# Rotary embedding: the first store queued after half, not a quarter, of the last load

## The chip, the core and the metric

The kernel runs on one core of one Trainium2 chip. The metric is the device time in microseconds (us) from start to end of the program. The core has five engines; this kernel computes on VectorE (DVE in the profile) and a little on ScalarE (ACT). GpSimd (POOL), SyncE (SP) and ScalarE issue transfers, and 16 DMA engines carry them between the chip's main memory (HBM) and the on-chip memory of 128 partitions. TensorE is not used.

## The reference

The input `x` is float32 with 8 batches, 8 heads, 1024 positions and 64 features. Each pair of features (i, i + 32) is rotated by an angle, position times frequency i.

```python
half = x.shape[-1] // 2
angles = np.outer(positions, freqs)
cos = np.cos(angles)
sin = np.sin(angles)
x_first, x_second = x[:, :, :, :half], x[:, :, :, half:]
out_first = x_first * cos - x_second * sin
out_second = x_first * sin + x_second * cos
return np.concatenate([out_first, out_second], axis=-1).astype(np.float32)
```

The tensor is 16.8 MB and is read once and written once, so that at least 33.6 MB pass through HBM.

## The kernel before, in words

The 64 pairs of batch and head ("heads") are cut into groups. One group is 8 heads: each head's 1024 positions are cut into 16 chunks of 64 positions, and the 8 x 16 chunks fill the 128 partitions, each with one contiguous row of `run` = 64 x 64 = 4096 values. `groups` holds seven such groups (heads 8 to 63) and, last, a group of `first` = 6 heads (heads 2 to 7), which fills 96 partitions. Heads 0 and 1 (`edge` = 2) are held apart: they are loaded first, as float32, through SP's hardware queue, computed last, and stored by SP at the very end (L176).

The groups are loaded by software DMAs that POOL issues (L83). They read float32 and write bfloat16 into the tiles `xt`. The seven full groups are one load of 1024 KB each; the last group's load is cut into two loads at `cut = first_part`, the columns before the cut and the columns from it. There is one `xt` tile and one output tile `ot` for every group, so no tile is used twice and no load waits for a tile. POOL issues eight loads at once; the ninth, the second part of the last group, is issued at 11.68 us, once the first load has landed.

VectorE and ScalarE build a table of sines (with both signs) and cosines once (`tables`). Then `rotate` makes three VectorE instructions for each group: the product with the sines into `t` (L139), the product with the cosines into `ot` (L140), and the sum of `ot` and `t` with swapped halves (L142). After the third group a second, smaller table is built for the two edge heads (`turnsr`, `wholer`, `sinr`, `cosr`).

The results go out through POOL too (L152), as software DMAs that read bfloat16 and write float32, one for each group. Loads and stores of POOL are in one queue, q0, and the order is the program's. Ahead of the first store the program has POOL wait until the first part of the last load is in:

```python
nc.gpsimd.keepalive_nop(ins=[nc.gpsimd.lower_ap(xts[-1][:, :first_part])])
```

So all stores stand behind this one wait, although the first groups are computed long before it is met. The stores follow in the order of the groups, each after its group's L142. SP's two stores of the edge heads are issued once all stores but the last one have landed (`stored[:-1]`).

Of the kernel before, what the change touches and what calls it, by code (L numbers as in the profile page):

```python
# [10 lines left out]
def kernel(  # L11
# [29 lines left out]
    run = C * d  # L41
# [31 lines left out]
    nc.scalar.dma_start(out=fr[0:P:32], in_=freqs[None, :].to_broadcast([P // 32, half]))  # L73


    first_part = run // 4
    xts = []
    for lo, n in groups:
        xt = xpool.tile([P, run], bf16, name="xt")[:n * chunks]
# [130 lines left out]
```

## Time and profile before

| what | us |
|---|---|
| median of 6 runs | 86.17 |
| the six runs | 86.51, 86.58, 84.47, 85.24, 86.28, 86.07 |
| the profiled execution | 86.51 |
| its span in the trace | 84.5 |
| VectorE busy | 65.2 |
| ScalarE busy, POOL busy | 9.4, 9.4 |
| first store issued (L152) | 42.55 |
| last VectorE instruction ends (L167) | 74.1 |
| SP issues the edge heads' stores (L176) | 78.75 |

The span is the time from the first to the last record of the trace, and all times of the trace count from its start. The profiled execution took 2.0 us more than its span. Its sizes for software transfers are those of the on-chip side for loads (bfloat16, half of what HBM gives) and those of the HBM side for stores. A transfer's time to landing counts from its issue to the moment when its semaphore says that all of it is there; a transfer spreads over the 16 DMA engines and has landed when the slowest of them is done. A DMA share is the mean over the 16 engines, so that 1/16 = 0.06 is one engine at work; the shares can pass 1, since the packets of an engine overlap a little.

### The profile page before, as it was taken

How to read it: one execution, taken by the hardware profiler on the slowest of the kernel's cores; microseconds unless marked ns; L12 is line 12 of the kernel's file. 1: busy time of each engine (PE TensorE's matmuls, PEld its weight loads, DVE VectorE, ACT ScalarE, POOL GpSimd, SP SyncE). 2: the span in 40 equal slices, each digit the busy share in tenths (PEclk: the TensorE clock that was granted, in tenths of full speed). 3: DMA queues.
4: the chain of work that ended last, by engine and by line, in shares of the span. 5: the costliest groups of instructions: out<-in, count | busy, mean ns of one | idle time of the engine just before them, and what ended most of it. 6: DMA issues, size and time to landing. Idle time of an engine off the chain costs nothing.

```text
span 84.5 us, 155 instructions
## 1 busy us (share of the span) xinstructions
DVE 65.2 (77%) x46; ACT 9.4 (11%) x8; POOL 9.4 (11%) x22
## 2 busy tenths in 40 slices
DVE  0122998299999999999999999999999999900000
ACT  0600001999000000000006000000000000000000
POOL 5960020000000000000072000200200200200000
DMA  2999999999999999999859999999999999999981
GB/s 21 316 202 206 217 209 225 206 213 217 211 219 214 221 209 225 206 196 181 177 213 411 427 442 427 442 411 458 372 496 372 496 372 496 372 496 372 496 319 61
DMA packets 3112, 25.45 MB, mean 301 GB/s; under 512 B 504, under 2 KB 520, under 8 KB 1224
## 3 DMA queue, kind: packets, MB, share of 16 engines
q0 software_dynamic: 2352, 24.38, 94.4%
q1 hardware_dynamic: 576, 1.05, 3.8%
q10 hardware_dynamic: 184, 0.02, 0.3%
HBM read 16.79 MB, written 16.78 MB: 397 GB/s over the span
## 4 chain that ended last, share of the span: by engine, by line
DVE 65%; issue 12%; DMA 7%; ACT 2%; ACTq 1%
DVE ot L140 21%; DVE ot L142 16%; DVE t L139 14%; DMA const<-in_freqs_dram 7%; DVE turnsc L102 3%; DVE turnsc L96 3%; ACT sinc L106 2%; DVE wholec L100 1%; DVE last L167 1%; DVE last L164 1%; DVE sinc L107 1%; DVE t L164 1%; ACTq L70 1%; DVE turnsr L102 0%; DVE turnsr L96 0%
## 5 line engine op out<-in xcount | busy, mean ns | idle before, releaser
L139 DVE TENSOR_TENSOR t<-xt,sinc 128x4096 bf16<-128x4096 bf16 (+1 forms) x8 | 18.2, 2288 | 0.0
L140 DVE TENSOR_TENSOR ot<-xt,cosc 128x4096 bf16<-128x4096 bf16 (+1 forms) x8 | 18.2, 2288 | 0.0
L142 DVE TENSOR_TENSOR ot<-ot,t 128x4096 bf16<-128x4096 bf16 (+1 forms) x8 | 18.2, 2286 | 0.0
L152 POOL DMA_DIRECT2D out_dram<-ot x8 | 4.3, 534 | 55.9 <-DVE wholer L100 30.2
L83 POOL DMA_DIRECT2D xt<-in_x_dram x9 | 4.9, 571 | 6.9 <-DMA xt<-in_x_dram 6.1
L106 ACT ACTIVATE sinc<-turnsc 128x2048 bf16<-128x2048 f32 x1 | 1.9, 1909 | 10.5 <-DVE turnsc L102 10.5
L106 ACT ACTIVATE sinr<-turnsr 128x256 bf16<-128x256 f32 x1 | 0.4, 416 | 23.4 <-DVE turnsr L102 23.4
L89 DVE LOAD_MASK_SELECT const<-const x1 | 0.0, 14 | 3.0 <-DMA const<-in_freqs_dram 3.0
L102 DVE TENSOR_TENSOR turnsc<-turnsc,wholec 128x2048 f32<-128x2048 f32 x1 | 2.3, 2293 | 0.0
L96 DVE TENSOR_TENSOR turnsc<-pos_f,fturn 128x2048 f32<-128x2048 f32 x1 | 2.3, 2292 | 0.0
L107 DVE TENSOR_SCALAR sinc<-sinc 128x2048 bf16<-128x2048 bf16 x1 | 0.7, 695 | 2.0 <-ACT sinc L106 2.0
L88 DVE LOAD_MASK_SELECT const<-const x1 | 0.0, 14 | 2.8 <-DMA const<-in_positions_dram 2.8
L110 ACT ACTIVATE cosc<-wholec,half_pi 128x2048 bf16<-128x2048 f32 x1 | 2.0, 2002 | 0.1
L109 ACT ACTIVATE wholec<-turnsc 128x2048 f32<-128x2048 f32 x1 | 1.9, 1893 | 0.0
L106 ACT ACT_TABLE_LOAD x1 | 1.3, 1283 | 2.6 <-issue 2.6
L167 DVE TENSOR_TENSOR last<-last,t 128x1024 f32<-128x1024 f32 x1 | 1.2, 1226 | 0.0
L100 DVE TENSOR_SCALAR wholec<-turnsc 128x2048 f32<-128x2048 f32 x1 | 1.2, 1226 | 0.0
L164 DVE TENSOR_TENSOR last<-x,cosr 128x1024 f32<-128x1024 bf16 x1 | 1.2, 1208 | 0.0
L127 ACT CAST x<-xf 128x1024 bf16<-128x1024 f32 x1 | 1.0, 1028 | 0.0
L116 DVE CAST pos_f<-const 32x64 f32<-32x64 int32 x4 | 0.8, 203 | 0.1
L64 DVE MEMSET const<- 128x160 int32 x1 | 0.2, 192 | 0.8 <-PEq L194 0.8
L110 ACT ACTIVATE cosr<-wholer,half_pi 128x512 bf16<-128x512 f32 x1 | 0.7, 722 | 0.0
(15 smaller groups left out, 3.8 us busy)
## 6 DMA issues: line engine op xcount, KB each, us to landing
out_dram<-ot POOLq DMA_DIRECT2D x7, 2048.0 KB, 13.4
xt<-in_x_dram POOLq DMA_DIRECT2D x7, 1024.0 KB, 23.1
out_dram<-ot POOLq DMA_DIRECT2D x1, 1536.0 KB, 10.4
xt<-in_x_dram POOLq DMA_DIRECT2D x1, 576.0 KB, 32.9
xf<-in_x_dram SPq DMA_DIRECT2D x2, 256.0 KB, 2.9
out_dram<-last SPq DMA_DIRECT2D x2, 256.0 KB, 4.3
xt<-in_x_dram POOLq DMA_DIRECT2D x1, 192.0 KB, 36.9
const<-in_positions_dram ACTq DMA_DIRECT2D x1, 8.0 KB, 2.6
```

The lines of the kernel that those rows point to most:

```text
L83: nc.gpsimd.dma_start(out=xt[:, a:b], in_=hbm(x, lo, n, a, b))
L96: v.tensor_mul(out=turns, in0=pos_f.to_broadcast([P, n, half]), in1=fturn.to_broadcast([P, n, half]))
L100: v.tensor_scalar(out=whole, in0=turns, scalar1=magic, scalar2=magic, op0=Alu.add, op1=Alu.subtract)
L102: v.tensor_sub(out=turns, in0=turns, in1=whole)
L106: nc.scalar.activation(out=sin[:, :, 0], in_=turns, func=Act.Sin, scale=twopi)
L110: nc.scalar.activation(out=cos, in_=whole[:, :, None, :].to_broadcast([P, n, copies, half]), func=Act.Sin, scale=-twopi, bias=half_pi)
L139: v.tensor_mul(out=t.rearrange(flat), in0=xt, in1=sin_c[:n].rearrange(flat))
L140: v.tensor_mul(out=ot, in0=xt.rearrange("p (c two h) -> p c two h", two=2, h=half), in1=cos_c[:n].to_broadcast([n, C, 2, half]))
L142: v.tensor_add(out=ot, in0=ot, in1=swap(t))
L152: nc.gpsimd.dma_start(out=hbm(out, lo, n), in_=ot.rearrange("p c two h -> p (c two h)")))
L164: v.tensor_mul(out=o, in0=x0, in1=w.rearrange("p r two h -> p (r two h)")[:, None, :].to_broadcast(flat))
L167: v.tensor_add(out=last.rearrange(rows, two=2, h=half), in0=last.rearrange(rows, two=2, h=half), in1=swap(t.rearrange(rows, two=2, h=half)))
```

## The change

`first_part` becomes half of a row instead of a quarter. A row has 4096 values, 64 positions of 64 features. The last group's two loads were 1024 and 3072 columns wide (16 and 48 positions, 192 KB and 576 KB on chip); they become 2048 columns each (32 positions, 384 KB). The same variable names the columns for which POOL waits ahead of the first store, so this wait is now for the first 2048 columns. Nothing else changes, and the instructions on every engine keep their order.

```diff
-    first_part = run // 4
+    first_part = run // 2
     xts = []
     for lo, n in groups:
         xt = xpool.tile([P, run], bf16, name="xt")[:n * chunks]
         cut = first_part if lo == groups[-1][0] else run
         for a, b in ((0, cut), (cut, run)):
             if a < b:
                 nc.gpsimd.dma_start(out=xt[:, a:b], in_=hbm(x, lo, n, a, b))
```

## The prediction

> **What bounds the kernel now.** I read the page's slices first, then the DMA queues over the second half of the span, then half-microsecond windows around the turn from loading to storing, and last the landing times of the two parts of the last load.
>
> ```profile
> DVE 65.2 (77%) x46; ACT 9.4 (11%) x8; POOL 9.4 (11%) x22
> ...
> DMA  2999999999999999999859999999999999999981
> ```
>
> The slices are 2.1 us wide. VectorE (DVE) is the busiest engine at 77%, and the chain that ended last names it, but VectorE is done at 74.1 us while the span ends at 84.5. The 16 DMA engines are busy from end to end, with one dip ("85", slices 20 and 21). So the kernel is a run of loads, a turn, and a run of stores. The view of the DMA queues from 43.66 to 83.7 us shows the second run:
>
> ```profile
> q0 software_dynamic: 1122, 16.26, 100.0%
> q1 hardware_dynamic: 288, 0.52, 3.5%
> ```
>
> The stores fill the 16 engines from the turn to the end, 16.78 MB with no gap to absorb a delay. Whatever moves the moment at which the last DMA engine begins to store moves the end by the same amount. The windows (VectorE, ScalarE and POOL busy, clock, DMA share, GB/s) show that moment:
>
> ```profile
> 41.50:42.00 0.50, 0.50 (x3) 0.00 (x0) 0.00 (x0) 1.00 0.67 135
> 42.00:42.50 0.50, 0.50 (x1) 0.00 (x0) 0.00 (x0) 1.00 0.26 49
> 42.50:43.00 0.50, 0.50 (x1) 0.00 (x0) 0.45 (x1) 1.00 0.06 12
> 43.00:43.50 0.50, 0.50 (x1) 0.00 (x0) 0.50 (x2) 1.00 0.06 12
> 43.50:44.00 0.50, 0.50 (x1) 0.00 (x0) 0.50 (x2) 1.00 1.23 504
> ```
>
> A share of 0.06 is one engine in sixteen. From 42.6 us fifteen engines have finished all their loads and stand idle; one trails and still loads. The page's list of DMA issues gives the landings, counted from the issue:
>
> ```profile
> xt<-in_x_dram POOLq DMA_DIRECT2D x1, 576.0 KB, 32.9
> ...
> xt<-in_x_dram POOLq DMA_DIRECT2D x1, 192.0 KB, 36.9
> ```
>
> The first part (192 KB, issued near 5.0 us) lands at 41.9, the second (issued at 11.68) at 44.6. A part lands when its slowest engine is done, so both are times of the trailing engine. The seventh full load (issued near 4.5, 36.2 us to landing) lands at 40.75. On the trailing engine the first part therefore took 41.9 - 40.75 = 1.15 us and the second 44.6 - 41.9 = 2.7 us, which is 0.9 per quarter.
>
> ```profile
> 41.91 2.29 DVE L142 TENSOR_TENSOR ot<-ot,t 128x4096 bf16<-128x4096 bf16 x1
> 42.55 1.61 POOL L152 DMA_DIRECT2D out_dram<-ot  x3 [30.25 <-DVE wholer L100]
> ```
>
> The three outputs that POOL stores here were ready by then (the third L142 ends at 39.3), so POOL waits for the landing of the first part, not for L100. From landing (41.9) to the start of the issue is 0.65 us. The first store packets start at 43.7, 1.1 us after that, so from landing to first packet is 1.8 us. The trailing engine starts its last load packet at 43.84 and, at its pace of one packet in 0.455 us, is free at 44.3, and then stores. Its 44.3, not the 43.7 of the others, sets the end. The store wake thus has some 0.6 us to spare on the engine that counts.
>
> **The change part by part.**
>
> *Issues.* Nine software loads and eight stores stay, in the same order, with the same 96 rows in each part, so POOL's issues (0.53 to 0.57 us each) cost nothing more. The first part grows from 2 KB to 4 KB a row (bf16), the second shrinks from 6 to 4. SP, ScalarE and VectorE keep their instructions. VectorE first needs the last load at 62.2 us, 17 us after it lands. Cost 0.
>
> *The wait.* POOL now waits for half of the last load. On the trailing engine that half is six rows. From below, at the pace of the 6 KB rows, it takes 2 x 0.9 = 1.8 us; from above, at the pace of the 2 KB rows, 2 x 1.15 = 2.3. The excess of the 2 KB rows (0.25 us in six) is a cost by the row more likely than by the byte, since the 6 KB rows show none, so I take 1.9. The half lands at 40.75 + 1.9 = 42.65, which is 0.75 later than 41.9. Behind the waiting instruction on POOL stand all eight stores: the first three are ready, the fourth is ready at 44.2 and issued at 44.49 now. The first three move by 0.75, the fourth by less. No DMA engine waits for the fourth, since each engine then holds three stores of about 4.8 us (landings lie 4.9 us apart).
>
> *What hides it.* First store packet: 42.65 + 1.8 = 44.45. Load end on the trailing engine: now 44.3; with two parts at 1.9 instead of 1.15 + 2.7 it is 0.05 earlier, 44.25. The later of the two decides: 44.45 against 44.3 now, so +0.15. The cover was 0.6 us, the delay is 0.75, and what sticks out is paid. The idle of the fifteen others grows by 0.75 each and costs nothing, as they were some 0.5 us ahead of the trailing one to the end.
>
> *Bounds.* From below: half at 1.8, landing 42.55, first packet 44.35, loads done by 44.1: +0.05; if the wake is also 0.2 us quicker (it is one sample), -0.15. From above: half at 2.3, landing 43.05, first packet 44.85, but loads end at 44.3 + 2 x 2.3 - 3.85 = 45.05: +0.75. I take +0.15, being nearer to the row with large rows.
>
> *A rule that speaks against it.* The Trainium skill (DMA: Bandwidth & Descriptors, Anatomy of one DMA) puts about 2 us of fixed cost on a software DMA, most of it the receipt of the last byte before the semaphore moves. If the half were reported nearly 2 us after its last packet, the store would start at about 42.3 + 2.0 + 1.75 = 46.05: all cover would be gone, both before and after, and the change would cost its full +0.75. The trace's row says 0.3 us here: the second part's last packet ends at 44.3 and it lands at 44.6. I take the row, and +0.15.
>
> *A second one.* The skill (SBUF — State Buffer, Who interferes with whom) says that a VectorE instruction in a two-port mode shuts GpSimd out of the port through which it writes software DMA descriptors, for the whole instruction. By the rule alone a wake that falls into a bad VectorE instruction costs up to its 2.29 us. The row: the first issues run 42.55 to 44.16 inside L142's 41.91 to 44.20 and still take 0.53 each. Moved by 0.75 the first lies in the same L142 (43.3 to 43.85), and those after it meet L102 and L139, tensor-tensor forms too. I take 0.
>
> **The sum.** +0.15 us against the profiled execution: its 86.51 would be 86.66. That execution lies 0.34 above the median of 86.17 of the runs shown, so the forecast is 86.17 + 0.15 = 86.3. The six runs lie from 84.47 to 86.58, which I read as an engine trailing by more or less. A measurement of this kernel can tell about 2% (1.7 us) from no change.
>
> **The rivals.**
>
> *Hidden but for a rest (the forecast), 55%.* 86.3; by the bounds 86.0 to 86.9.
>
> *The full delay is paid, 25%.* If in the timed runs no engine trails at the turn, the first packet of the stores decides on all sixteen. Place: the dip at 42 to 44.5 us. Price: the delay of the landing, 0.75, up to 0.95 with the slower rows: 87.0. For it: fifteen engines do stand idle for over a microsecond. Against it: with even engines the wake has cover too, as the second part then still lasts 1.8 us after the first lands and the wake takes 1.8. It decides from the point where the trailing engine ends its loads before the first store packet is ready.
>
> *The wake meets VectorE's port, 6%, the slower side.* Place: POOL's first L152 issue. Price: held to the end of L142 at 44.2, first packet at 45.35: +1.05; held through L102 and L139 to 46.7 it is 47.85: +3.55, 89.7. For it: VectorE is busy without a break there. Against it: the row above. It decides once an issue at L152 lasts over 0.6 us.
>
> *A gain, 12%.* The 2 KB rows vanish (-0.25 of load on every engine) and the wake is quick: -0.15, 86.0. More is only to be had if the trailing engine trails less in the changed kernel: the best run shown, 84.47, is where that ends, which is 2% off. Nothing in the edit reaches the early loads, where the lag is already 2 us (the first load is 10.1 us to landing, the later ones 4.9 apart).
>
> *It doesn't do what it says, 2%.* The wait may be met by other work. The instruction order shows two 96x2048 loads and the wait in its old place, so no.
>
> **How the numbers follow.** The likeliest is 86.3. The scatter of single runs is wider than every cost here. Low end: the fast runs shown plus the sum, 84.47 + 0.15 = 84.6. High end: the full delay on the slowest run, 86.58 + 0.9 = 87.5. The likeliest case's own range is 86.0 to 86.9. Chances: slower by over 2% needs the port rival (0.06), or timed runs that trail more, and more often, than those before (0.14): 0.2. Faster by over 2% needs the trailing engine to be gone in most runs: 0.1. Within 2%: 0.7.
>
> **What would show it.** The first L152 issue should start at 43.3 (+-0.2), the 384 KB first part should land at 42.65, its second part near 44.6, one-engine windows (0.06) should run from 42.6 to 44.2, and all sixteen engines should start storing together near 44.45. Stores then last as long as before. I am wrong if the first issue moves by over 1.2 us, if an L152 issue lasts longer than 0.6 us, if the second part lands after 45, or if the store run from first packet to end changes by over 0.3 us.

## The result and the profile after

| | before | after |
|---|---|---|
| median over all runs, us | 85.67 (72 runs) | 84.99 (35 runs) |
| lowest and highest run, us | 84.30 and 87.03 | 84.42 and 87.25 |
| the profiled execution, us (span) | 86.51 (84.5) | 86.37 (84.2) |

The ratio of after to before is 0.9984, with a 95% interval from 0.996 to 1.0007: no difference that this comparison can tell. Single executions of both kernels scatter over almost 3 us, and each ratio to the kernel before in this document compares only those runs of a kernel that lie within 1.5% of its quickest. Over all runs the means are 85.66 and 85.51 us, and the difference lies between -0.5 and +0.25 us (95%, by resampling the runs), so that neither a small gain nor the +0.15 of the forecast is excluded. The two medians, 0.7 us apart, are not evidence. The 35 runs of the changed kernel fall into two clumps, 21 from 84.42 to 85.28 us and 14 from 85.72 to 87.25, and their median stands near the edge of the first. In five groups of runs the kernel before had medians of 85.67, 85.96, 85.56, 85.59 and 85.52, and the changed kernel in a second group of six runs had 86.56. What makes this scatter is part of what follows.

On the page of the changed kernel the row of DMA shares has its dip in the same place (slice 21, "5"), and it ends full:

```profile
DMA  2999999999999999999959999999999999999993
```

The half-microsecond windows at the turn from loads to stores (VectorE, ScalarE, POOL busy, clock, DMA share, GB/s) differ from those of before:

```profile
41.50:42.00 0.50, 0.50 (x1) 0.00 (x0) 0.00 (x0) 1.00 1.02 205
42.00:42.50 0.50, 0.50 (x1) 0.00 (x0) 0.00 (x0) 1.00 0.59 115
42.50:43.00 0.50, 0.50 (x1) 0.00 (x0) 0.25 (x1) 1.00 0.49 98
43.00:43.50 0.50, 0.50 (x1) 0.00 (x0) 0.50 (x2) 1.00 0.21 41
43.50:44.00 0.50, 0.50 (x3) 0.00 (x1) 0.50 (x2) 1.00 1.10 459
```

No single engine trails here. A share of 0.49 is about half of the sixteen engines; these end their loads between 43.0 and 43.6, and then all sixteen start to store together, between 43.9 and 44.0. The list of DMA issues, taken for the loads issued from 5.0 us on, gives the seventh full load and the first half, and taken from 9 us on, the second half:

```profile
xt<-in_x_dram POOLq DMA_DIRECT2D x1, 1024.0 KB, 35.8
xt<-in_x_dram POOLq DMA_DIRECT2D x1, 384.0 KB, 37.0
...
xt<-in_x_dram POOLq DMA_DIRECT2D x1, 384.0 KB, 32.7
```

With issues at 4.5, 5.04 and 11.2 us they land at 40.3, 42.07 and 43.9. On the engines that come last, the half took 1.77 us. The timeline around POOL's first stores:

```profile
41.34 2.29 DVE L142 TENSOR_TENSOR ot<-ot,t 128x4096 bf16<-128x4096 bf16 x1
42.75 2.13 POOL L152 DMA_DIRECT2D out_dram<-ot  x4 [30.90 <-DMA xt<-in_x_dram]
43.54 0.42 DVE L102 TENSOR_TENSOR turnsr<-turnsr,wholer 128x256 f32<-128x256 f32 x1
43.87 2.29 DVE L139 TENSOR_TENSOR t<-xt,sinc 128x4096 bf16<-128x4096 bf16 x1
```

The releaser is now named rightly, the load into `xt`. Four issues take 2.13 us, 0.53 each, across L142, L102 and L139.

### The profile page after: what moved, and what is told of

Its sections match the earlier page's. It is cut to its first block, busy times and chain, and to the rows that moved or that the text cites. A ratio compares the mean times of both kernels' runs of the same rounds, so it can differ in the third digit from the quotient of the medians.

```text
span 84.2 us, 155 instructions
## 1 busy us (share of the span) xinstructions
DVE 65.1 (77%) x46; ACT 9.4 (11%) x8; POOL 9.4 (11%) x22
## 3 DMA queue, kind: packets, MB, share of 16 engines
q1 hardware_dynamic: 576, 1.05, 3.7%
## 4 chain that ended last, share of the span: by engine, by line
DVE 65%; issue 12%; DMA 7%; ACT 2%; ACTq 1%
DVE ot L140 21%; DVE ot L142 16%; DVE t L139 14%; DMA const<-in_freqs_dram 7%; DVE turnsc L102 3%; DVE turnsc L96 3%; ACT sinc L106 2%; DVE wholec L100 1%; DVE last L167 1%; DVE last L164 1%; DVE sinc L107 1%; DVE t L164 1%; ACTq L70 1%; DVE turnsr L102 0%; DVE turnsr L96 0%
## 5 line engine op out<-in xcount | busy, mean ns | idle before, releaser
L139 DVE TENSOR_TENSOR t<-xt,sinc 128x4096 bf16<-128x4096 bf16 (+1 forms) x8 | 18.2, 2288 | 0.0
L142 DVE TENSOR_TENSOR ot<-ot,t 128x4096 bf16<-128x4096 bf16 (+1 forms) x8 | 18.2, 2286 | 0.0
L102 DVE TENSOR_TENSOR turnsc<-turnsc,wholec 128x2048 f32<-128x2048 f32 x1 | 2.3, 2293 | 0.0
## 6 DMA issues: line engine op xcount, KB each, us to landing
out_dram<-ot POOLq DMA_DIRECT2D x1, 1536.0 KB, 10.7
```

The lines of the kernel that those rows point to most:

```text
L102: v.tensor_sub(out=turns, in0=turns, in1=whole)
L139: v.tensor_mul(out=t.rearrange(flat), in0=xt, in1=sin_c[:n].rearrange(flat))
L142: v.tensor_add(out=ot, in0=ot, in1=swap(t))
```

## The experiments

**The rule that was tested.** "Cover" is the prediction's own theory: the wake of POOL is hidden as long as an engine that still loads ends later than the first store could start. From the span of a profile subtract the start of POOL's first store issue. If the wake of POOL sets the start of the last engine's stores, this is a constant, since everything after it is the fixed run of stores. If a load's end sets it, the remainder is longer than the constant.

| kernel | span | first store issue | remainder |
|---|---|---|---|
| after (half) | 84.2 | 42.75 | 41.5 |
| d_half | 83.7 | 42.27 | 41.4 |
| d_threeq | 84.0 | 42.55 | 41.5 |
| d_whole | 87.0 | 45.53 | 41.5 |
| r_rows (half) | 83.0 | 41.51 | 41.5 |
| p_hold (half) | 84.0 | 42.53 | 41.5 |
| x_late (half) | 84.1 | 42.64 | 41.5 |
| x_late_h (half) | 84.1 | 42.59 | 41.5 |
| x_late_t (three quarters) | 84.9 | 43.41 | 41.5 |
| x_split (half) | 83.5 | 42.02 | 41.5 |
| x_pool_h (half) | 83.9 | 42.37 | 41.5 |
| before (quarter) | 84.5 | 42.55 | 41.95 |
| x_late_q (quarter) | 83.5 | 41.54 | 42.0 |
| x_split_q (quarter) | 83.3 | 41.30 | 42.0 |
| x_pool_q (quarter) | 83.3 | 41.34 | 42.0 |
| d_eighth | 84.7 | 42.31 | 42.4 |
| x_late_e (eighth) | 83.5 | 41.09 | 42.4 |

The remainder is 41.5 wherever POOL waits for a half or more, within the rounding of the page, however late the issue is. With a quarter it is 0.5 longer, with an eighth 0.9. So the wake decides from the half on and the loads' end below it; the knee lies between a quarter and a half. This is the prediction's cover, read directly.

The same can be read from the other side. From the end of the last load packet to the end of the span it is 40.2 us in all six profiles with a quarter or an eighth, 40.6 in the eight with a half, 41.5 with three quarters and 42.5 with the whole. The half therefore leaves a hole of about 0.4 us behind the last load, in the changed kernel (43.58 to 84.23 us, 40.65) as in x_late_h (43.48 to 84.07, 40.59), with or without an engine that trails.

### The length of the wait in the kernel itself

Five versions differ only in `first_part` or in what POOL waits for.

**d_half** is the changed kernel again.

> The changed kernel again. Theory (cover): the end follows the later of two moments on the DMA engines that load longest: their load end (44.3 us in the profile of before) and the landing of the first part plus 1.8 us. Half landing late, the second wins by little: +0.1 to +0.3 us against before, 0.1 to 0.4%. Rival (paid in full): each delay of the landing is paid: +0.75 us, 0.9%. Rival (evening out): a later first store lets the DMA engines finish level and saves time: -0.7 us, 0.8%, as the medians of all runs differ.

Measured: six runs from 84.5 to 86.74 us, median 86.56. These are too few to give a ratio. Its trace gives the row in the table above.

**d_eighth**

```diff
-    first_part = run // 2
+    first_part = run // 8
```

> First part an eighth of a row (8 of 64 positions), the wait with it. Cover: the landing is 0.5 us earlier than before, but the load end decides already: 0.0 us, at most +0.1 for the 1 KB rows. Paid in full: -0.5 us (0.6% faster). Evening out: slower than before, +0.3 us or more.

Measured: 1.0032, from 0.9982 to 1.0082, 22 runs. Paid in full (0.994) is outside the interval; cover (1.000 to 1.001) is inside.

**d_threeq**

```diff
-    first_part = run // 2
+    first_part = 3 * run // 4
```

> First part three quarters of a row (48 of 64 positions), the wait with it. Cover: on the DMA engine that loads longest the part lands 0.9 us after the half does, so the first store packet comes about 0.9 us after that engine's load end; +0.9 to +1.1 us against before, 1.1 to 1.3%. In its own trace the span should be the first store packet plus 40.2 to 40.4 us. Paid in full from a quarter on: +1.9 us, 2.2%. Evening out: not slower than before.

Measured: 1.0118, from 1.0028 to 1.0209. That is +1.0 us of some 85, as cover has it; "paid in full" (1.022) and "evening out" (1.000 or less) fall outside. Its windows show engines with nothing to do:

```profile
42.00:42.50 0.50, 0.50 (x1) 0.00 (x0) 0.00 (x0) 1.00 0.07 12
42.50:43.00 0.50, 0.50 (x1) 0.00 (x0) 0.45 (x1) 1.00 0.00 0
43.00:43.50 0.50, 0.50 (x1) 0.00 (x0) 0.50 (x2) 1.00 0.00 0
43.50:44.00 0.50, 0.50 (x3) 0.00 (x0) 0.50 (x2) 1.00 1.25 524
```

A share of 0.00 for over a microsecond is a stop of all sixteen, which the profile of before doesn't have at the turn.

**d_whole**

```diff
-    nc.gpsimd.keepalive_nop(ins=[nc.gpsimd.lower_ap(xts[-1][:, :first_part])])
+    nc.gpsimd.keepalive_nop(ins=[nc.gpsimd.lower_ap(xts[-1])])
```

> Cut at half, but POOL waits for both halves ahead of the first store. Cover: first store packet at 44.6 + 1.8 = 46.4 in the time of the profile of before, against a load end of 44.3: all cover gone, +2.0 us, 2.3%, with all sixteen DMA engines idle for about 1.8 us. Paid in full: +2.8 us, 3.2%. Evening out: not slower than before by more than 0.5 us.

Measured: 1.0257, from 1.0112 to 1.0403, +2.2 us. The six runs don't separate cover (2.3%) from paid in full (3.2%), since both lie in the interval. The trace does: its remainder of 41.5 is 0.5 below that of a quarter, so that 0.5 us of the later issue is not paid. The stop is what was expected, about 2 us of nothing (44.55 to 46.65 us):

```profile
44.00:44.50 0.50, 0.50 (x1) 0.00 (x0) 0.00 (x0) 1.00 0.05 8
44.50:45.00 0.50, 0.50 (x2) 0.00 (x0) 0.00 (x0) 1.00 0.00 0
45.00:45.50 0.50, 0.50 (x3) 0.06 (x1) 0.00 (x0) 1.00 0.00 0
45.50:46.00 0.50, 0.50 (x1) 0.50 (x2) 0.47 (x1) 1.00 0.00 0
46.00:46.50 0.50, 0.50 (x1) 0.47 (x2) 0.50 (x2) 1.00 0.00 0
46.50:47.00 0.50, 0.50 (x1) 0.42 (x1) 0.50 (x2) 1.00 1.25 524
```

These are the wake and the first store's own latency with no cover at all. The "evening out" theory ends here.

**n_nowait** takes the line with the wait out altogether; the cut stays at half.

> Cut at half, and the wait ahead of the first store is left out, so that POOL issues each store when its group is computed (first at about 28 us). Cover: stores queue behind the loads on each DMA engine, each engine goes on to stores with no gap, the end is the load end of the longest engine: 0.0 to -0.2 us against before. Paid in full: -1.8 us (2.1% faster), since the dip closes. Evening out: slower, +0.5 us or more, as engines that load early start storing while the others still load.

Measured: 1.0124, from 1.0021 to 1.0227, on six runs from 84.98 to 87.30. Cover missed here by about 1 us in this ratio; the means of all runs are 86.13 against 85.80 us. The gain that "paid in full" expects did not come either. The trace has no dip at the turn, and from the end of the last load packet (43.67) to the end of the span it is 40.2 us, as cover has it for a wake that comes early enough. What is longer is the load:

```profile
40.50:41.00 0.50, 0.50 (x3) 0.00 (x0) 0.00 (x0) 1.00 1.05 156
41.00:41.50 0.50, 0.50 (x1) 0.00 (x0) 0.00 (x0) 1.00 1.37 180
```

The engines are at least as busy as in the changed kernel, which has shares of 1.01 and 1.02 and moves 205 GB/s in both windows, and move less. In this trace 37 of the last load's 192 packets take up to 0.75 us between 40.2 and 42.2 us, in place of 0.32, some 0.55 us for each engine on average; in the eight other profiles whose last load is cut into halves none does. So stores queued early may slow the end of the loads. That is one trace, and six runs with a scatter of 2.3 us don't settle what the wait earns; this stays open.

### The size of the rows

**r_rows** keeps the wait for half and gives it the old small rows:

```diff
-        cut = first_part if lo == groups[-1][0] else run
-        for a, b in ((0, cut), (cut, run)):
-            if a < b:
+        cuts = (0, run // 4, run // 2, run) if lo == groups[-1][0] else (0, run)
+        for a, b in zip(cuts, cuts[1:]):
+            if a < b:
```

> The wait of the changed kernel (half of the last load) with rows of the old size: three loads of 16, 16 and 32 positions, POOL waits for the first two. Cover with a price on 2 KB rows (0.25 to 0.3 us for each quarter on an engine): the half lands 0.5 us later than with 4 KB rows, and the end follows: +0.4 to +0.6 us against the changed kernel, 0.5 to 0.7% against before. If the wait alone counted and the row size did not: 0.0 against the changed kernel.

Measured: 1.0023, from 0.9984 to 1.0061, against 0.9984 for the changed kernel. The 0.4% between the two has the sign of a price on 2 KB rows and nearly its size, but the intervals overlap. Not settled by this run; the level pairs and the single packets, below, say more.

### What scatters the runs

In the profile of before one engine trailed at the turn, in that of after about half of them did. The lag is there from the first load on. If it could be removed, the change would show without it. Four edits try it on the changed kernel, some of them also with a quarter.

**p_hold** has POOL issue only two loads before the first has landed:

```diff
         xts.append(xt)
+        if len(xts) == 2:
+            nc.gpsimd.keepalive_nop(ins=[nc.gpsimd.lower_ap(xts[0])])
```

> The changed kernel, but POOL issues only two loads at the start and the other seven once the first has landed. It asks why some DMA engines trail by 1 to 2 us from the first load on. If POOL's writing of descriptors for further loads (until 5.6 us) slows the engines' first packets: the lag at the landing of the first load shrinks to under 0.5 us, some lag may come back at 9 to 13 us when POOL issues the rest, and the median falls by 0.5 to 1.5 us with the spread. If the slow start has another cause: lag, median and spread as in the changed kernel, within 0.3 us.

Measured: 1.000, from 0.9956 to 1.0043; 22 runs from 84.39 to 87.36, median 86.69. The lag is still there. The list of DMA issues, taken for 1.0 to 1.4 us, gives the first load's time from issue to landing:

```profile
xt<-in_x_dram POOLq DMA_DIRECT2D x1, 1024.0 KB, 9.4
```

In this kernel POOL issues nothing between 2.5 and 11.2 us, so descriptors written for the third and later loads are not what holds the first load up.

**x_late** has SP load the two edge heads only when the first group is in:

```diff
-    for i in range(edge):
-        nc.sync.dma_start(out=xf[:, i], in_=hbm_head(x, i))
...
+    nc.sync.keepalive_nop(ins=[nc.sync.lower_ap(xts[0])])
+    for i in range(edge):
+        tc.keep_in_program_order(nc.sync.dma_start(out=xf[:, i], in_=hbm_head(x, i)))
```

> The changed kernel, but SP loads the two edge heads only once the first software load has landed (about 9 us), so that no hardware-queue transfer of size stands ahead of the software loads at the start. If the meeting of both queues slows the engines' first packets: the lag at the first load's landing shrinks to under 0.5 us and the median falls by 0.5 to 1.5 us. If not: lag and spread as before; the bytes are the same, so the end moves by less than 0.3 us.

Measured: six runs from 86.05 to 86.26 us. The scatter is gone, 0.2 us instead of almost 3, but the level is 1.0157 (1.0113 to 1.0201) of before by the ratio, and by the means of all runs 0.5 us above it (86.15 against 85.61). The first load now takes 8.1 us, as the view of the `xt` tile shows for the repeat (x_late_h); the smallest of the times from issue to landing is the first load's here:

```profile
DMA to landing us min/median/max: 8.1/26.9/36.9
```

The same view of before has 10.1 there, that of after 9.7. The fall of the median that was expected did not come. The price is at the start; windows of 2 us of x_late_h, and then of the changed kernel:

```profile
2.00:4.00 2.00, 1.05 (x5) 1.28 (x1) 2.00 (x5) 1.00 0.81 82
4.00:6.00 2.00, 0.06 (x1) 0.00 (x0) 1.61 (x4) 1.00 0.98 201
```

```profile
2.00:4.00 2.00, 0.18 (x2) 1.28 (x1) 2.00 (x5) 1.00 1.04 297
4.00:6.00 2.00, 0.73 (x4) 0.00 (x0) 1.62 (x4) 1.00 0.91 139
```

Without SP's loads the stretch from 2 to 4 us moves 82 instead of 297 GB/s; from 4 to 6 us it is 201 against 139. The lower window is not an idle one: its share is 0.81. The software packets start at 2.6 us there and not at 3.6, and they are slow. The trace of x_late_h has 15 load packets of over 0.9 us, the longest 1.95, between 2.6 and 3.7 us; 0.62 us is usual. The traces of the six other profiles without SP's loads have 13 to 20, about one for each engine, all begun by 4.0 us. With SP's loads the count changes from one execution to the next, from none (r_rows) and 2 (before) to 12 (the changed kernel, between 3.8 and 6.4 us) and 17 (d_eighth). So the edit does not take the slow first packets away. It seems to give one to nearly every engine, which would keep them level and explain why the level is no lower; which packet ran on which engine the trace does not say.

**x_split** leaves one edge head at the start and moves the other; **x_split_q** is the same with a quarter:

```diff
-    for i in range(edge):
-        nc.sync.dma_start(out=xf[:, i], in_=hbm_head(x, i))
+    nc.sync.dma_start(out=xf[:, 0], in_=hbm_head(x, 0))
...
+    nc.sync.keepalive_nop(ins=[nc.sync.lower_ap(xts[0])])
+    tc.keep_in_program_order(nc.sync.dma_start(out=xf[:, 1], in_=hbm_head(x, 1)))
```

> The changed kernel with one edge head loaded at the start, as before, and the other only after the first software load. If it is the meeting of both queues at the start that scatters the engines, and one head's 256 KB just fills the time until the first software packets: the runs lie within 0.5 us of each other near the best of the changed kernel, 84.4 to 84.9 us, and the median falls by about 1 us against before. If any hardware transfer at the start does it: spread and median as in the changed kernel.

> The same with first_part = run // 4: a second pair for the change. Cover: 0.0 +- 0.15 us against x_split. Paid in full: 0.75 us faster. Row size alone: 0.3 us slower.

Measured: x_split from 85.07 to 87.44 us, x_split_q from 84.84 to 86.94, 22 runs each, 1.0074 (1.0037 to 1.0111) and 1.0101 (1.0058 to 1.0144) of before. One head is enough to bring the scatter back, so the hope of having both was wrong. As a pair for the change these two say nothing.

**x_pool_h** and **x_pool_q** put the edge heads into POOL's own queue, behind the first group, with a half and a quarter:

```diff
-    for i in range(edge):
-        nc.sync.dma_start(out=xf[:, i], in_=hbm_head(x, i))
...
         xts.append(xt)
+        if len(xts) == 1:
+            for i in range(edge):
+                tc.keep_in_program_order(nc.gpsimd.dma_start(out=xf[:, i], in_=hbm_head(x, i)))
```

> The changed kernel, with the two edge heads loaded by POOL's software queue behind the first group, so that SP moves no data at the start. If the meeting of the queues makes the scatter: runs within 0.5 us of each other, near 85.6 us (the first data flow 0.9 us later than before, and nothing else changes). If not: a scatter of 2 us or more.

> The same with first_part = run // 4. Cover: 0.3 to 0.5 us faster than x_pool_h, as in the first pair (x_late_q against x_late_h, 0.38). Row size alone: 0.3 us slower.

Measured: x_pool_h 22 runs from 85.67 to 86.03 us, x_pool_q 22 runs from 85.26 to 86.22. The kernel before ran from 84.15 to 86.90 in its 59 runs beside them. Two different ways of taking SP's loads away from the start remove most of the scatter, and leaving half of them does not.

### The change in kernels that start level

These kernels resolve what the original hides.

> The kernel of x_late again (wait for half, edge heads loaded by SP after the first software load), as the partner of x_late_q on the same chip. Its runs should again lie within about 0.3 us of each other, near 86.1 us.

> The same with first_part = run // 4, so that the pair is the change itself in kernels whose DMA engines start level. Cover: with 2 KB rows the loads end about 0.3 us later than in the partner, and with the earlier wake no engine waits for stores; in the partner the stores start about 0.3 us after the loads end. The two cancel: 0.0 +- 0.15 us between the pair. Paid in full: the quarter is 0.75 us faster than the half. Row size alone: the quarter is 0.3 us slower.

> As x_late_q, with first_part = run // 8. Cover: the loads' end decides with a quarter already, so an earlier wake brings nothing: 85.7 us, 0.0 +- 0.15 us against x_late_q (85.71). If every step of the wait costs (0.38 us from a quarter to a half): about 0.2 us faster, 85.5.

> As x_late_h, with first_part = 3 * run // 4. Cover: past the knee each further quarter of the last load is paid whole, 0.9 us: 86.1 + 0.9 = 87.0 us. If each quarter costs 0.4 us: 86.5.

The edits are those of x_late with `first_part` a half, a quarter, an eighth and three quarters of `run`.

| wait for | us, median (lowest to highest), runs | step |
|---|---|---|
| an eighth | 85.59 (85.40 to 86.16), 22 | |
| a quarter | 85.71 (85.45 to 85.74), 8 | +0.1 |
| a half | 86.09 (85.85 to 86.31), 6 | +0.4 |
| three quarters | 86.96 (86.65 to 87.18), 6 | +0.9 |

The eighth and the three quarters ran on another chip than the pair of quarter and half, so that their steps also hold what the chips differ by: the kernel before had means of 85.62 and 85.56 us there. They came as cover had it (85.7 and 87.0). The pair of half and quarter ran on the same chip and doesn't overlap: 86.09 / 85.71 = 1.0045, 95% interval 1.002 to 1.007 by resampling the runs. The expectation of 0.0 +- 0.15 us was wrong, and so was "row size alone". "Paid in full" was wrong too: the delay of the wake is 42.59 - 41.54 = 1.05 us in the two traces, and 0.4 is paid. The knee is where cover puts it, and the step past it is paid whole. The pair x_pool_h and x_pool_q has the same sign and less of it, 85.86 / 85.72 = 1.0016, from 0.9995 to 1.0033. This interval includes no difference, and the step of 0.14 us is below the 0.3 to 0.5 us that were expected.

The windows of x_late_h, wait for half:

```profile
42.50:43.00 0.50, 0.50 (x2) 0.00 (x0) 0.41 (x1) 1.00 0.59 115
43.00:43.50 0.50, 0.50 (x2) 0.18 (x1) 0.50 (x2) 1.00 0.06 8
43.50:44.00 0.50, 0.50 (x1) 0.50 (x2) 0.50 (x2) 1.00 1.25 524
```

and of x_late_q, wait for a quarter:

```profile
42.50:43.00 0.50, 0.50 (x2) 0.00 (x0) 0.50 (x2) 1.00 1.10 340
43.00:43.50 0.50, 0.50 (x2) 0.19 (x1) 0.42 (x2) 1.00 1.05 426
43.50:44.00 0.50, 0.50 (x1) 0.50 (x2) 0.27 (x1) 1.00 1.04 426
```

With a quarter the stores are queued when the loads end, and the share doesn't fall under 1 in these windows: each engine goes over on its own, which is why the GB/s climb step by step. With a half the share falls to 0.06 for half a microsecond and then all engines start at once. That hole is the cost, and it is the 0.4 us between the two rests behind the last load packet (40.59 and 40.20 us). With the change the kernel has no version among these that beats the one before: the level ones scatter less but start more than 1 us above its best runs.

## Why the prediction was right or wrong

**What bounds the kernel: right.** The remainder of 41.5 us in eleven profiles, whatever POOL waits for from a half on, is the fixed run of stores.

**Cover: right in form.** The end follows the later of the loads' end and the wake. An eighth gains nothing, a half sticks out by a little, three quarters and the whole are paid from the knee on (+1.0 and +2.2 us in the kernel itself).

**The step that failed: the base.** The forecast is a level, 86.17, plus 0.15, and the level was the wrong term. 86.17 is the median of six runs; 72 runs put it at 85.67. The prediction said that the scatter of the runs is an engine trailing by more or less, and then took the median of six such draws as a level from which to count 0.15. The changed kernel's median came out at 84.99, 1.3 us below the forecast of 86.3 and below its likeliest range of 86.0 to 86.9, and a second group of six runs of it at 86.56. Which clump the median falls into is luck, and the clumps lie some 2 us apart, more than everything that was being summed. In the profiles with a half or less the span ends 40.6 or 40.2 us after the slowest engine's last load packet, and when that packet ends changes from one execution to the next. The kernels that start level, whose runs agree within 0.2 to 1.0 us, show the change itself as +0.4 and +0.14 us.

**The sum of +0.15: two terms mis-sized.** The first is the hole. The prediction had the first store packet at 44.45 and the loads' end at 44.25, a hole of 0.2 us. The hole was about 0.4 us in every profile with a half. In the changed kernel the loads end 1.5 us after the half lands, not 1.6, and the last of the sixteen engines begins to store 0.15 us after the first one does, which took the 1.8 us of the prediction. For the same reason the prediction's remark that level engines have cover too is wrong: it set 1.8 us from landing to landing against the wake, but the engines are done 0.3 us before the second landing.

The second is the price of 2 KB rows. The prediction took 1.15 us for the quarter, let six such rows cost 0.25 us more than larger ones, and so let the half win back most of what it waits. In x_late_q the seventh load lands at 40.0 (issue 4.5, 35.5 to landing) and the quarter at 40.9 (5.04, 35.8): 0.9 us, no excess. The half takes 1.77 in the changed kernel, not 1.9. The excess in the profile of before belonged to that execution. Without it nothing offsets the half's hole, and the +0.15 became +0.4 and +0.14 us in the two level pairs. Both lie inside the stated bounds of -0.15 and +0.75.

**What stays open.** The kernel's own ratio, 0.9984 and at most 1.0007, lies a little below the forecast's 1.0017, and below both level pairs. A saving through larger rows, present only where engines start unevenly, would explain it. Two windows of before, the first amid the 2 KB rows of the first part and the second behind them, show what could be saved:

```profile
38.50:39.00 0.50, 0.50 (x1) 0.00 (x0) 0.00 (x0) 1.00 1.09 131
40.50:41.00 0.50, 0.50 (x1) 0.00 (x0) 0.00 (x0) 1.00 1.12 229
```

Of the 96 packets of the first part, 45 took longer than the 0.17 us that all 96 take in x_late_q, up to 0.43, some 0.4 us for each engine on average; where the last load is cut into halves and POOL waits, no packet of it is slowed in any of the eight profiles. But these are single executions, the same count gives less than 0.1 us in x_split_q and r_rows, and in d_threeq it is 16 of the 6 KB packets that are slowed, so size alone is not the cause. It isn't shown that such a saving holds over the runs, and the mean of all runs leaves room for a cost.

**What the profile should have shown: half missed.** The first issue came at 42.75, not 43.3, and the second half landed at 43.9, not 44.6, since in this execution the seventh load landed 0.45 earlier and the half took 0.13 less. The one-engine windows were not there. That all sixteen start to store together, 1.8 us after the landing, was right, as was an issue of 0.53 us.

**The rivals.** *Paid in full* fell with the eighth and with the level pair. *VectorE's port* fell: the four issues of 0.53 us lie across L142, L102 and L139 in the trace of after, all of them tensor-tensor instructions; other forms did not run beside an issue here. The rule on the receipt that the prediction weighed (the Trainium skill, DMA: Bandwidth & Descriptors, Anatomy of one DMA: about 2 us of fixed cost) would, by the prediction's estimate, have the loads' end followed by 3.75 us before a store flows; d_whole, which has no cover at all, shows 2.1.

## What to carry to other kernels

A transfer queued behind a wait cost nothing here as long as the wait was met earlier than the queue ran dry by the whole latency from landing to store, 1.8 us for the first engine and 1.95 for the last. Work that latency out in your kernel, and place the trigger just ahead of it, at the slowest DMA engine. Read that engine from short windows: a DMA share of 1/16 is one engine at work, and 0.00 is the hole that is paid. Compare the share with the GB/s beside it: a full share at few GB/s means slow packets, not idle engines. Before a tenth of a per cent is argued over, find out what scatters the single runs; a variant that removes the scatter, even a slower one, shows the change that the original hides.

## What the runs showed of the hardware

With SP's hardware-queue loads at the very start, beside POOL's first software loads, the DMA engines fall out of step, differently in each execution, and stay so to the end of the loads: in the profile of before fifteen engines are done with their loads by 42.6 us and the last at 44.3, while in x_late_h all sixteen end between 42.8 and 43.5. The first load takes 9.1 to 10.7 us to landing in the executions profiled with that lag, and 7.9 to 8.3 in the others, among them two that had both of SP's loads (d_threeq, r_rows). Without these loads the runs of one kernel lie within 0.2 to 1.0 us, with them within 2.1 to 3.3 us. Slow first packets, 0.9 to 2 us in place of 0.62, are there in both cases; without SP's loads there are 13 to 20 of them in each profile, with both of them none to 17. Taking the loads away therefore gains nothing on average: with a quarter the means are 85.66 (x_late_q) and 85.56 us (before, on the same chip). Why the first packets of the software queue are slow was not found; POOL's writing of descriptors for the third and later loads is excluded by p_hold.
